# Hybrid decoder block on one core: when roundings, sums, gates and splits are given out in the branch and output stages

## The chip, the core and the metric

The kernel runs on one core of a Trainium2 chip. TensorE (PE in the profile) multiplies, VectorE (DVE), ScalarE (ACT) and GpSimd (POOL) do the elementwise work, and SyncE (SP) issues most transfers; POOL and ACT issue some too. Each engine takes its instructions in order. The metric is the device time of one execution in microseconds; the median of the runs stands for a kernel.

## The reference, cut to what matters

The input of 512 positions gets 16 meta tokens in front and a layer norm. One projection gives ten groups of 1024 columns: queries, keys, values and gates of two attention branches, and a merge gate for each. After the attentions:

```python
br_d = einsum('blw,wd->bld', y_d * silu(g_d), w_br_diff[i])
br_s = einsum('blw,wd->bld', y_s * silu(g_s), w_br_sb[i])
merged = sigmoid(m_d + b_gate[i, 0]) * br_d + sigmoid(m_s + b_gate[i, 1]) * br_s
y = einsum('bld,de->ble', merged, w_out[i])
h = layer_norm(DN_ALPHA * h + y, ln_g[i], ln_b[i])
return h[:, N_META:]
```

Everything is float32, 1024 wide. The attentions and their projections come first and take some 526 us; the change is behind them.

## The kernel before

**Products in two halves.** TensorE multiplies rounded operands (type fp32r). Each float32 operand is therefore split into a rounded part (ACT casts it) and the remainder (DVE subtracts), and a product is three matmuls: high by high, low by high, high by low. For weights these are `wh` and `wl`, a "half" of 128x512 each. `hi(h)` casts and `lo(h)` subtracts half number h; `prep(h)` does both, and each step of the products calls it for the half that is four ahead (AHEAD = 4). `fetch` has SP load raw weights as ring buffers come free (6 of `raw`, 4 of `rawa`).

**Gates.** A merge gate `md` j or `ms` j is one product of 24 matmuls of 512 columns (two halves of weights), then a sigmoid on ACT. MD and MS are the results, 128x512 each, j = 0 to 7.

**Branch products.** Each branch is computed two output blocks at a time by a scheme with seven products in place of eight: a "pair" BD p (differential branch) or BS p (stick-breaking), p = 0 to 3. A product has 12 matmuls of 256 columns. The operands are seven combinations of quarters of y, built in four parts by `operands` (results `gh` and `gl`, sums in `t`); the weights need five loads per pair, two with a second matrix added while it is loaded (POOL's accumulating transfers into `rawa`), and two sums on DVE. `pair` accumulates products in PSUM bank x, copies x away on ACT in between (u, then w), and DVE combines them (c11, c22, c21) and multiplies with the gate. PE may write x again only when it has been copied or read.

**Merge.** `merged(j)` adds MD to MS on DVE, casts the sum (`mh`, ACT), subtracts (`ml`, DVE). It is called at the end of the products of BS p for j = 2p + 1 and 2p.

**Output.** `split_out(c, k)` splits 128 rows of w_out for column half c into `wo0h`/`wo0l` or `wo1h`/`wo1l`. For each half and each of four position blocks t, 24 matmuls of 512 columns give `pso` (the last block in two of 256). DVE builds the residual in `hr` (two instructions a block and half, from x loaded once more), adds pso, takes statistics, and normalizes after the second half. `load_half` loads x and the vectors into the buffers of wh and wl.

**Order.** In these stages the order of each engine, SP's too, is that of the program text: `keep_order` chains them. `seq` fixes the order of products; `run(products, steps)` inserts other work at given points of progress, in rough us. Before, it was: md3 to md7, BD0 to BD3, ms0 to ms3, BS0, ms4, BS1, ms5, ms6, ms7, BS2, BS3, output. Lines that the steps of the prediction touch: L162 `wh`, L167 `wl`, L153 `sum`, L139 accumulating transfers, L856 to L862 operands, L884 u, L892 c22, L917 to L921 merge, L927 and L928 w_out, L960 and L961 residual, L985 addition, L450 to L452 gates, L879 pairs, L982 to L984 output.

Of the kernel before, what the change touches and what calls it, by code (L numbers as in the profile page):

```python
# [43 lines left out]
def hybrid_block_kernel(ctx: ExitStack, tc: tile.TileContext, x, meta, emb_g, emb_b, w_in, b_gate,  # L44
# [24 lines left out]
    for u, (kind, n) in enumerate(UNITS):  # L69
        if u + 1 < len(UNITS):  # L70
# [39 lines left out]
    raws, split, adds = {}, [], []  # L110
    rings = {False: ("raw", 6, []), True: ("rawa", 4, [])}
    state = {"l": 0, "h": 0, "sum": None, "n": 0}
# [6 lines left out]
    def fetch(most=99):  # L119

        while state["l"] < len(loads) and most:
            l = state["l"]
            src, more = loads[l]
            tag, bufs, log = rings[more is not None]
            if len(log) >= bufs and left[log[-bufs]] or (more is not None) not in pools:
                return
            raw = pools[more is not None].tile([P, 4, P], F32, tag=tag, name=tag, bufs=bufs)
            nc.sync.dma_start(raw if l < WOUT else raw.rearrange("p a b -> p (a b)"), src)
            if more is not None:
                adds.append((state["n"], l, more))  # L130
            raws[l] = raw
            log.append(l)
            state["l"] += 1
            most -= 1

    def add_up(now):
        while adds and (now is None or adds[0][0] <= now):
            _, l, more = adds.pop(0)
            g.dma_start(raws[l], more, accum_op=ALU.add)  # L139

    def hi(h):

        assert len(split) == h
        item = items[h]
        for l in item if isinstance(item, tuple) else [item]:
            assert l not in [l for _, l, _ in adds], "not added up yet"
        if item is None:
            raw = raw0[:, h // 2, ts(h % 2, 4)]
        elif isinstance(item, tuple):
            first, second = item  # L150
            one = state["sum"] if first is None else raws[first]
            raw = one if first is None else pools[True].tile([P, 4, P], F32, tag="sum", name="sum", bufs=2)
            v.tensor_tensor(raw, one, raws[second], op=ALU.add)  # L153
            for l in item:
                if l is not None:
                    left[l] -= 1
            state["sum"] = raw
        else:
            raw = raws[item]
        wh, wl = [wpool.tile([P, 4, P], F32R, tag=w, name=w, bufs=6) for w in ("wh", "wl")]  # L160
        split.append((raw, wh, wl))
        s.copy(wh, raw)  # L162
# [685 lines left out]
    def operands(y):  # L848


        gh, gl = [lp.tile([P, 7, 4, 256], F32R, tag=n, name=n) for n in ("gh", "gl")]

        def part(i):
            a, b = y[:, i, :], y[:, i + 4, :]
            t = [lp.tile([P, 256], F32, tag="tmp", name="t", bufs=8) for n in range(4)]
            v.tensor_tensor(t[0], a[:, LEFT], a[:, RIGHT], op=ALU.subtract)  # L856
            v.tensor_tensor(t[2], a[:, RIGHT], b[:, RIGHT], op=ALU.subtract)
            v.tensor_tensor(t[1], t[2], a[:, LEFT], op=ALU.subtract)
            v.tensor_tensor(t[3], t[1], b[:, LEFT], op=ALU.add)
            for n, src in enumerate((a[:, LEFT], b[:, LEFT], b[:, RIGHT], *t)):  # L860
                s.copy(gh[:, n, i, :], src)
                v.tensor_tensor(gl[:, n, i, :], src, gh[:, n, i, :].bitcast(F32), op=ALU.subtract)  # L862

        return (gh, gl), [lambda i=i: part(i) for i in range(4)]

    def pair(kind, p, G, t, done):
# [5 lines left out]
        u, z7, w, c11, c22, c21 = [lp.tile([P, 256], F32, tag="tmp", name="t", bufs=8) for n in range(6)]  # L872
# [35 lines left out]
    SS = ypool.tile([P, KT, S], F32, tag="yd", name="ss")  # L908
# [5 lines left out]
    def merged(j):  # L914

        t = SS[:, j, :]
        v.tensor_tensor(t, t, MD[j], op=ALU.add)  # L917
        pool, tag, bufs = (gpool, "sg", 6) if j < 3 else (lp, "td", 5)
        MH[j] = pool.tile([P, S], F32R, tag=tag, name="mh", bufs=bufs)
        s.copy(MH[j], t)  # L920
        v.tensor_tensor(ML[:, j, :], t, MH[j].bitcast(F32), op=ALU.subtract)  # L921
# [10 lines left out]
    for p in range(4):  # L932
        steps = []
        if p == 2:
            run([merge_gate(1, j, SS[:, j, :]) for j in (6, 7)])
        if p == 3:
            WO = [[hpool.tile([P, KT, 512], F32R, tag=f"hT{x}", name=f"wo0{x}") for x in "hl"]]
            steps = [(1.5 + 1.2 * k, lambda k=k: split_out(0, k)) for k in range(6)]
        run([pair("BS", p, G, [SS[:, 2 * p + m, :] for m in range(2)], lambda m, p=p: merged(2 * p + m))], steps)
        if p < 2:  # L940
            run([merge_gate(1, 4 + p, SS[:, 4 + p, :])])

# [19 lines left out]

    load_half(0)
    for k in range(6, KT):
        split_out(0, k)
    load_half(1)
    residual(0, 0)
    WO.append([lp.tile([P, KT, 512], F32R, tag=f"g{x}", name=f"wo1{x}") for x in "hl"])
    lgb = ypool.tile([P, 2, D], F32, tag="yd", name="lgb")
    nc.scalar.dma_start(lgb[:, 0, :], ln_g[0].partition_broadcast(P))  # L970
    nc.scalar.dma_start(lgb[:, 1, :], ln_b[0].partition_broadcast(P))
    sts = [lr.tile([P, 4, 6], F32, tag="fst", name="fst", bufs=4) for t in range(NB)]
    for c in range(2):
        for t in range(NB):
            st, final = sts[t], t == NB - 1
            for o, w in [(0, 256), (256, 256)] if final and c else [(0, 512)]:
                r, hr = ds(o, w), hrs[t][c]
                ps = pj.tile([P, 512], F32, tag="pj", name="pso")[:, :w]
                for n, k in enumerate((0, 1, 2, 3, 4, 5, 7, 6)):
                    mh, ml = MH[k][:, ts(t, P)], ML[:, k, ts(t, P)]  # L980
                    wh, wl = WO[c][0][:, k, r], WO[c][1][:, k, r]
                    pe.matmul(ps, mh, wh, start=(n == 0), stop=False)  # L982
                    pe.matmul(ps, mh, wl, start=False, stop=False)
                    pe.matmul(ps, ml, wh, start=False, stop=(n == KT - 1))  # L984
                v.scalar_tensor_tensor(hr[:, r], hr[:, r], DN_ALPHA, ps, op0=ALU.mult, op1=ALU.add)  # L985
# [64 lines left out]
```

## Time and profile before

| | |
|---|---|
| median of three runs | 749.88 us (746.13 to 750.96) |
| profiled execution, its own time | 746.05 us |
| its span | 744.2 us |
| mean granted TensorE clock | 0.995 |
| bytes read / written | 67.32 / 2.10 MB |

The page gives for each engine its busy time and share of the span. A window row gives the same for a stretch. A timeline row reads: start, duration, engine, line, operation, output <- inputs, shapes, count, and in brackets how long the engine was idle before it and what ended that. "wh", "q" and the like are the program's tile names. A releaser is what came last by the profile; the engine may have been held in turn by something else, which its own rows show.

### The profile page before, as it was taken

How to read it: one execution, taken by the hardware profiler on the slowest of the kernel's cores; microseconds unless marked ns; L12 is line 12 of the kernel's file. 1: busy time of each engine (PE TensorE's matmuls, PEld its weight loads, DVE VectorE, ACT ScalarE, POOL GpSimd, SP SyncE). 2: the span in 40 equal slices, each digit the busy share in tenths (PEclk: the TensorE clock that was granted, in tenths of full speed). 3: DMA queues.
4: the chain of work that ended last, by engine and by line, in shares of the span. 5: the costliest groups of instructions: out<-in, count | busy, mean ns of one | idle time of the engine just before them, and what ended most of it. 6: DMA issues, size and time to landing. Idle time of an engine off the chain costs nothing.

```text
span 744.2 us, 13129 instructions
## 1 busy us (share of the span) xinstructions
PE 722.2 (97%) x4658; PEld 659.0 (89%) x4658; DVE 586.1 (79%) x1342; ACT 448.6 (60%) x1131; POOL 85.1 (11%) x110
## 2 busy tenths in 40 slices
PE   9999999999999999999999999999999999998985
PEld 8999999999999897989999999988878989997765
DVE  6798778877785699796969696976498898748697
ACT  5686777877776776665657575665375564444300
POOL 3310111011000000000000100110022011110002
PEclk9999999999999999999999999999999999999999
DMA  9142221222213222222222231222188484563802
GB/s 273 51 119 81 62 82 47 69 58 85 66 50 85 71 72 57 57 86 57 72 72 78 65 86 58 78 64 85 44 155 183 102 198 100 141 144 119 291 15 100
DMA packets 120483, 70.27 MB, mean 94 GB/s; under 512 B 4145, under 2 KB 114898, under 8 KB 120418
## 3 DMA queue, kind: packets, MB, share of 16 engines
q1 hardware_dynamic: 111650, 64.18, 29.6%
q0 software_dynamic: 8448, 4.20, 4.6%
q10 hardware_dynamic: 320, 1.06, 0.4%
q8 instruction: 37, 0.61, 0.3%
q14 instruction: 28, 0.23, 0.1%
HBM read 67.32 MB, written 2.10 MB: 93 GB/s over the span
## 4 chain that ended last, share of the span: by engine, by line
PE 84%; DVE 10%; DMA 2%; issue 1%; ACT 1%; POOL 1%; SPq 0%; DVEq 0%; ACTq 0%; POOLq 0%
PE ps L466 23%; PE ps L450 10%; PE ps L451 10%; PE ps L452 10%; PE q L879 10%; PE sc L608 4%; PE t L621 3%; DMA hr<-in_x_dram 2%; DVE wl L167 1%; PE t L626 1%; PE bank L341 1%; DVE gl L862 1%; PE av L784 1%; PE tv L571 1%; PE av L785 1%
## 5 line engine op out<-in xcount | busy, mean ns | idle before, releaser
L167 DVE TENSOR_TENSOR wl<-raw,wh 128x512 fp32r<-128x512 f32 x180 | 125.7, 705 | 38.0 <-ACT wh L162 35.9
L466 PE MATMUL ps<-hTh,wh 128*128 128x264 f32 x512 | 147.1, 287 | 0.0
L466 PE MATMUL ps<-hTl,wh 128*128 128x264 f32 x512 | 146.4, 286 | 0.0
L466 PE MATMUL ps<-hTh,wl 128*128 128x264 f32 x512 | 146.0, 285 | 0.0
L452 PE MATMUL ps<-hTh,wl 128*128 128x512 f32 x368 | 144.5, 393 | 1.1 <-DVE wl L167 1.1
L450 PE MATMUL ps<-hTh,wh 128*128 128x512 f32 x368 | 144.7, 393 | 0.1
L451 PE MATMUL ps<-hTl,wh 128*128 128x512 f32 x368 | 144.6, 393 | 0.0
L162 ACT CAST wh<-raw 128x512 fp32r<-128x512 f32 x180 | 110.0, 620 | 46.8 <-PE ps L451 36.0
L466 PEld LDWEIGHTS ps<-hTh,wh 128*128 128x128 f32 x512 | 96.4, 188 | 1.3
L466 PEld LDWEIGHTS ps<-hTl,wh 128*128 128x128 f32 x512 | 96.5, 188 | 0.9
L466 PEld LDWEIGHTS ps<-hTh,wl 128*128 128x128 f32 x512 | 96.4, 188 | 0.3
L452 PEld LDWEIGHTS ps<-hTh,wl 128*128 128x128 f32 x368 | 69.2, 188 | 15.1 <-DVE wl L167 1.5
L450 PEld LDWEIGHTS ps<-hTh,wh 128*128 128x128 f32 x368 | 69.2, 188 | 13.8 <-ACT wh L162 0.6
L451 PEld LDWEIGHTS ps<-hTl,wh 128*128 128x128 f32 x368 | 69.2, 188 | 12.9
L879 PE MATMUL q<-gh,wh 128*128 128x256 f32 x224 | 64.4, 287 | 5.2 <-ACT t L884 5.2
L879 PE MATMUL q<-gh,wl 128*128 128x256 f32 x224 | 64.2, 287 | 0.3 <-DVE wl L167 0.3
L879 PE MATMUL q<-gl,wh 128*128 128x256 f32 x224 | 64.0, 286 | 0.0
L632 DVE TENSOR_TENSOR al<-t,ah 128x512 fp32r<-128x512 f32 (+2 forms) x88 | 45.9, 526 | 19.9 <-ACT ah L631 13.5
L770 DVE TENSOR_TENSOR_SCAN om<-om 128x528 f32<-128x528 f32 (+2 forms) x64 | 55.0, 868 | 6.8 <-ACT om L766 6.4
L631 ACT CAST ah<-t 128x512 fp32r<-128x512 f32 (+2 forms) x88 | 39.9, 463 | 28.8 <-PE t L621 23.3
L608 PE MATMUL sc<-k,A 128*128 128x264 f32 (+2 forms) x256 | 56.5, 308 | 0.2 <-POOL k L525 0.2
L879 PEld LDWEIGHTS q<-gh,wh 128*128 128x128 f32 x224 | 43.7, 195 | 5.9 <-ACT t L884 5.6
(238 smaller groups left out, 1431.8 us busy)
## 6 DMA issues: line engine op xcount, KB each, us to landing
raw<-in_w_in_dram SPq DMA_DIRECT2D x152, 256.0 KB, 3.0
raw<-in_w_out_dram SPq DMA_DIRECT2D x16, 256.0 KB, 3.4
raw<-in_w_br_diff_dram SPq DMA_DIRECT2D x12, 256.0 KB, 3.8
raw<-in_w_br_sb_dram SPq DMA_DIRECT2D x12, 256.0 KB, 4.6
raw<-in_w_in_dram SPq DMA_DIRECT2D x4, 512.0 KB, 6.5
rawa<-in_w_br_diff_dram SPq DMA_DIRECT2D x8, 256.0 KB, 3.5
rawa<-in_w_br_diff_dram POOLq DMA_DIRECT2D x8, 256.0 KB, 5.8
rawa<-in_w_br_sb_dram SPq DMA_DIRECT2D x8, 256.0 KB, 4.4
```

The costliest lines, as they stand in the source:

```text
L162: s.copy(wh, raw)
L167: eng.tensor_tensor(wl, raw, wh.bitcast(F32), op=ALU.subtract)
L450: pe.matmul(ps, wh[:, k % 4, :], hTh[:, k, M:], start=(k == 0), stop=False)
L451: pe.matmul(ps, wh[:, k % 4, :], hTl[:, k, M:], start=False, stop=False)
L452: pe.matmul(ps, wl[:, k % 4, :], hTh[:, k, M:], start=False, stop=(k == KT - 1))
L466: pe.matmul(ps[:, :H2], a[:, k % 4, :], b[:, k, ts(c, H2)], start=(k == 0 and m == 0), stop=(k == KT - 1 and m == 2))
L608: pe.matmul(ps[:, :n], q, K[:, m, k0:k0 + n], start=(m == 0), stop=(m == 1))
L621: pe.transpose(t[:, o:o + P], a[:, AOFF[i] + j * P:AOFF[i] + (j + 1) * P], ident)
L631: s.copy(h, t[:, o:o + w])
L632: v.tensor_tensor(l, t[:, o:o + w], h.bitcast(F32), op=ALU.subtract)
L770: v.tensor_tensor_scan(rev, rev, rev, 1.0, ALU.mult, ALU.min)
L879: pe.matmul(bank, a[:, k, :], b[:, n, k, :], start=start and k == 0 and m == 0, stop=k == 3 and m == 2, skip_group_check=not start)
```

## The change

It does six things, all behind the attentions.

1. ms0 and ms1 move ahead of BD0; ms2 to ms6 stand ahead of BS0; BS0, BS1 and BS2 follow each other; ms7 stands between BS2 and BS3.
2. `operands` builds the four sums in one tile and casts and subtracts in three instructions of 256, 512 and 1024 columns instead of seven of 256; its four parts are spaced over seven gates (five in the second branch) instead of five (four). The pairs use slices of the same kind of tile.
3. The sums of weights (`add`) are computed one step before the half is cast.
4. For j below 6 the branch sum is an accumulating transfer on POOL's queue; its cast comes six steps of `prep` later and the remainder one more, from a list `later`. For j = 6 and 7 DVE adds, and the cast comes one step later.
5. Of the first half of w_out, five splits stand in BS3 (six before) and three behind it (two before).
6. In the output stage, splits of the second half and residuals are given out by a table, ahead of the addition of the block; the transfers of ln_g and ln_b are issued after the first block's splits.

```diff
-    seq += [("md", j) for j in range(3, 8)] + [("BD", p) for p in range(4)] + [("ms", j) for j in range(4)]
-    seq += [x for p in range(4) for x in ([("BS", p), ("ms", 4 + p)] if p < 2 else [("ms", 6), ("ms", 7), ("BS", 2)]
-                                          if p == 2 else [("BS", 3)])]
+    seq += [("md", j) for j in range(3, 8)] + [("ms", 0), ("ms", 1)] + [("BD", p) for p in range(4)]
+    seq += [("ms", j) for j in range(2, 7)] + [("BS", p) for p in range(3)] + [("ms", 7), ("BS", 3)]
...
+    def add(h):
+
+        first, second = items[h]
+        one = sums.pop(True) if first is None else raws[first]
+        raw = one if first is None else pools[True].tile([P, 4, P], F32, tag="sum", name="sum", bufs=2)
+        v.tensor_tensor(raw, one, raws[second], op=ALU.add)
...
     def prep(h):
         state["n"] += 1
-        add_up(state["n"] - 1)
         if h < len(items):
             hi(h)
             lo(h)
+        if h + 1 < len(items) and isinstance(items[h + 1], tuple):
+            add(h + 1)
         fetch()
+        while later and later[0][0] <= state["n"]:
+            later.pop(0)[1]()
...
-            for n, src in enumerate((a[:, LEFT], b[:, LEFT], b[:, RIGHT], *t)):
-                s.copy(gh[:, n, i, :], src)
-                v.tensor_tensor(gl[:, n, i, :], src, gh[:, n, i, :].bitcast(F32), op=ALU.subtract)
+            for o, src in ((slice(0, 1), a[:, LEFT].unsqueeze(1)), (slice(1, 3), b.rearrange("p (a n) -> p a n", a=2)),
+                           (slice(3, 7), t)):
+                s.copy(gh[:, o, i, :], src)
+                v.tensor_tensor(gl[:, o, i, :], src, gh[:, o, i, :].bitcast(F32), op=ALU.subtract)
...
-    run([merge_gate(0, j, MD[j]) for j in range(3, 8)], [(0.3 + 5.4 * i, f) for i, f in enumerate(parts)])
+    run([merge_gate(0, j, MD[j]) for j in range(3, 8)] + [merge_gate(1, j, early_ms[j]) for j in range(2)],
+        [(0.3 + 7.5 * i, f) for i, f in enumerate(parts)])
...
-    run([merge_gate(1, j, SS[:, j, :]) for j in range(4)], [(0.3 + 4.8 * i, f) for i, f in enumerate(parts)])
+    run([merge_gate(1, j, MS[j]) for j in range(2, 7)], [(0.3 + 5.5 * i, f) for i, f in enumerate(parts)])
...
     def merged(j):
-        t = SS[:, j, :]
-        v.tensor_tensor(t, t, MD[j], op=ALU.add)
-        pool, tag, bufs = (gpool, "sg", 6) if j < 3 else (lp, "td", 5)
-        MH[j] = pool.tile([P, S], F32R, tag=tag, name="mh", bufs=bufs)
-        s.copy(MH[j], t)
-        v.tensor_tensor(ML[:, j, :], t, MH[j].bitcast(F32), op=ALU.subtract)
+        wait = 6 if j < 6 else 1
+        if j < 6:
+            g.dma_start(MS[j], MD[j], accum_op=ALU.add)
+        else:
+            v.tensor_tensor(MS[j], MS[j], MD[j], op=ALU.add)
+        later.append((state["n"] + wait, lambda: rounded(j)))
+        later.append((state["n"] + wait + 1, lambda: rest(j)))
+        later.sort(key=lambda x: x[0])
...
-            steps = [(1.5 + 1.2 * k, lambda k=k: split_out(0, k)) for k in range(6)]
+            steps = [(0.8 + 1.6 * k, lambda k=k: split_out(0, k)) for k in range(5)]
...
-    residual(0, 0)
-    nc.scalar.dma_start(lgb[:, 0, :], ln_g[0].partition_broadcast(P))
-    nc.scalar.dma_start(lgb[:, 1, :], ln_b[0].partition_broadcast(P))
+    MEANWHILE = [[lambda: residual(0, 0)] + [lambda k=k: split_out(1, k) for k in range(3)],
+                 [lambda: residual(1, 0)] + [lambda k=k: split_out(1, k) for k in range(3, 6)],
+                 [lambda: residual(2, 0)] + [lambda k=k: split_out(1, k) for k in range(6, 8)] + [lambda: residual(0, 1)],
+                 [lambda: residual(3, 0)] + [lambda t=t: residual(t, 1) for t in range(1, 3)],
+                 [lambda: residual(3, 1)], [], [], []]
...
+                if o == 0:
+                    for work in MEANWHILE[NB * c + t]:
+                        work()
+                    if t == 0 and c == 0:
+                        nc.scalar.dma_start(lgb[:, 0, :], ln_g[0].partition_broadcast(P))
+                        nc.scalar.dma_start(lgb[:, 1, :], ln_b[0].partition_broadcast(P))
...
             if c == 0:
-                split_out(1, 2 * t)
-                split_out(1, 2 * t + 1)
-                if t + 1 < NB:
-                    residual(t + 1, 0)
-                residual(t, 1)
                 continue
```

Here `rounded(j)` is the cast of MS[j] to `mh` and `rest(j)` the remainder `ml`, as they stood in `merged` before.

**ACT, from the end of BS2 into BS3.** Before:

```order
L162 CAST wh<-sum 128x512
L920 CAST mh<-ss 128x512
L162 CAST wh<-raw 128x512
L920 CAST mh<-ss 128x512
L162 CAST wh<-rawa 128x512
L884 COPY t<-q 128x256
```

With the change, from the last two weight casts in BS2 through ms7 into BS3:

```order
L153 CAST wh<-sum 128x512
L153 CAST wh<-raw 128x512
L485 ACTIVATE ss<-ps,cols 128x512
L153 CAST wh<-rawa 128x512
L936 CAST wo0h<-raw 128x512
L880 COPY t<-q 128x256
L153 CAST wh<-raw 128x512
L936 CAST wo0h<-raw 128x512
L882 COPY t<-q 128x256
L153 CAST wh<-sum 128x512
L916 CAST mh<-ss 128x512
```

The copy u (L884 before, L880 now) no longer has the two casts of BS2's sums ahead of it; the first of them stands ten rows lower, and the first cast of w_out stands right ahead of u.

**DVE, from the last branch sum to the second block's residual.** `hr` is the residual, L960 and L966 its first instruction, L985 and L1002 the addition of the product. Before:

```order
L917 TENSOR_TENSOR ss<-ss,td 128x512
L921 TENSOR_TENSOR ml<-ss,mh 128x512
L928 TENSOR_TENSOR wo0l<-raw,wo0h 128x512 x2
L960 SCALAR_TENSOR_TENSOR hr<-hr,xmv,eg 128x512
L961 SCALAR_TENSOR_TENSOR hr<-hr,xrs,eb 128x512
L985 SCALAR_TENSOR_TENSOR hr<-hr,pso 128x512
L988 BN_STATS fst<-hr 128x6
L928 TENSOR_TENSOR wo1l<-raw,wo1h 128x512 x2
```

With the change:

```order
L927 TENSOR_TENSOR ss<-ss,td 128x512
L919 TENSOR_TENSOR ml<-ss,mh 128x512 x2
L937 TENSOR_TENSOR wo0l<-raw,wo0h 128x512 x3
L966 SCALAR_TENSOR_TENSOR hr<-hr,xmv,eg 128x512
L967 SCALAR_TENSOR_TENSOR hr<-hr,xrs,eb 128x512
L937 TENSOR_TENSOR wo1l<-raw,wo1h 128x512 x3
L1002 SCALAR_TENSOR_TENSOR hr<-hr,pso 128x512
L1005 BN_STATS fst<-hr 128x6
```

Three splits of the second half now stand ahead of the first block's addition, where two stood behind it.

**POOL, in the branch stages.** Before there are, behind the attentions' last gates, the sixteen accumulating transfers of weights and then the normalization:

```order
L481 TENSOR_TENSOR ysT<-sg,ysT 128x512 x2
L139 DMA rawa<-in_w_br_diff_dram 128x4x128 x8
L139 DMA rawa<-in_w_br_sb_dram 128x4x128 x8
L261 TENSOR_TENSOR lne<-fmv,epsr 128x1
L262 TENSOR_TENSOR frs<-lne,neghalf 128x1
```

With the change (`sm` and `ss` are MS, `sm` and `td` on the right MD):

```order
L129 DMA rawa<-in_w_br_diff_dram 128x4x128 x8
L129 DMA rawa<-in_w_br_sb_dram 128x4x128 x6
L925 DMA sm_6827<-sm_6702 128x512
L925 DMA sm_6826<-sm_6629 128x512
L129 DMA rawa<-in_w_br_sb_dram 128x4x128 x2
L925 DMA ss<-td 128x512
L925 DMA ss<-sm_6768 128x512
L925 DMA ss<-td 128x512 x2
```

Six transfers from one on-chip tile to another come in, the first two between the weight transfers of BS2 and those of BS3.

More of the change, by code (lines that the diff above doesn't have):

```diff
@@ L109, in hybrid_block_kernel @@
     raw0 = ypool.tile([P, 4, KT, P], F32, tag="ys", name="raw0")
-    raws, split, adds = {}, [], []
+    raws, split, sums, later = {}, [], {}, []
     rings = {False: ("raw", 6, []), True: ("rawa", 4, [])}
-    state = {"l": 0, "h": 0, "sum": None, "n": 0}
+    state = {"l": 0, "h": 0, "n": 0}
     pools = {False: wpool}
@@ L129, in fetch @@
             if more is not None:
-                adds.append((state["n"], l, more))
+                g.dma_start(raw, more, accum_op=ALU.add)
             raws[l] = raw
@@ L134, in fetch @@
             most -= 1
[L136 to L139, printed above, removed]
+    def add(h):
[3 more added lines that the diff above has]
+        v.tensor_tensor(raw, one, raws[second], op=ALU.add)
+        for l in items[h]:
+            if l is not None:
+                left[l] -= 1
+        sums[h] = sums[True] = raw
     def hi(h):
@@ L144, in hi @@
         item = items[h]
[L145 to L159, printed above, removed]
+        raw = raw0[:, h // 2, ts(h % 2, 4)] if item is None else sums.pop(h) if isinstance(item, tuple) else raws[item]
         wh, wl = [wpool.tile([P, 4, P], F32R, tag=w, name=w, bufs=6) for w in ("wh", "wl")]
@@ L871, in pair @@
         x, z, y = [pool.tile([P, 512], F32, tag=tag, name="q")[:, :256] for pool, tag in of]
-        u, z7, w, c11, c22, c21 = [lp.tile([P, 256], F32, tag="tmp", name="t", bufs=8) for n in range(6)]
+        tmp = lp.tile([P, 4, 256], F32, tag="tmp", name="t", bufs=2)
+        u, z7, w = c11, c22, c21 = [tmp[:, n, :] for n in range(3)]
         def product(q, bank, n, start=True):
```

32 lines of the change are left out of this document (19 added, 13 removed).

## The prediction

> **What bounds the kernel.** I read the page's engine table first, then windows by stage, then PE's timeline for every wait, and last ACT's and DVE's timelines around each.
>
> ```profile
> PE 722.2 (97%) x4658; PEld 659.0 (89%) x4658; DVE 586.1 (79%) x1342; ACT 448.6 (60%) x1131; POOL 85.1 (11%) x110
> ```
> PE is busy 97% of the span, and the change issues the same matmuls; only holes and slow stretches of PE can be won. All rows up to about 526 us stay in their order, so I look behind that. Columns of the next table, of windows: stretch in us, its length, PE busy (instructions), granted clock, DMA share, GB/s.
>
> ```profile
> 555.19:598.05 42.86, 40.81 (x337) 1.00 0.68 148
> 620.00:630.07 10.07, 10.07 (x86) 1.00 0.45 131
> 630.07:635.54 5.47, 5.47 (x27) 1.00 0.01 3
> 661.79:687.35 25.56, 22.07 (x169) 0.93 0.31 100
> 678.40:682.60 4.20, 4.20 (x22) 0.59 0.39 133
> 687.35:736.18 48.83, 44.73 (x218) 1.00 0.42 142
> 718.28:720.00 1.72, 1.72 (x8) 1.00 0.00 0
> ```
> An undisturbed pair (BS0, second row) takes 10.07 us, an undisturbed gate 5.47. By these, BD0 to BD3 (first row) lost 42.86 - 4 x 10.07 = 2.58. BS2 and BS3 (fourth) lost 25.56 - 20.14 = 5.42. The output product has seven blocks of 24 matmuls of 512 columns, as a gate has, and 48 of 256 columns, so it needs 7 x 5.47 + 48/84 x 10.07 = 44.04 and lost 4.79. The holes are these, by PE's timeline (start, duration, instruction, idle before and its releaser):
>
> ```profile
> 541.90 0.50 PE L452 MATMUL ps<-hTh,wl 128*128 128x512 f32 x1 [1.10 <-DVE wl L167]
> 557.33 0.39 PE L879 MATMUL q<-gh,wl 128*128 128x256 f32 x1 [0.30 <-DVE wl L167]
> 560.52 0.39 PE L879 MATMUL q<-gh,wh 128*128 128x256 f32 x1 [1.74 <-ACT t L884]
> 678.38 0.39 PE L879 MATMUL q<-gh,wh 128*128 128x256 f32 x1 [3.49 <-ACT t L884]
> 692.37 0.50 PE L982 MATMUL pso<-wo0h,mh 128*128 128x512 f32 x1 [0.75 <-ACT wo0h L927]
> 693.26 0.50 PE L983 MATMUL pso<-wo0l,mh 128*128 128x512 f32 x1 [0.39 <-DVE wo0l L928]
> 718.28 0.50 PE L983 MATMUL pso<-wo1l,mh 128*128 128x512 f32 x1 [2.97 <-DVE wo1l L928]
> ```
>
> **A. Two more gates ahead of BD0, fuller operand instructions.** DVE was the bound from 536 to 560: it took one operand part and two weight remainders (wl) in turn without a pause.
>
> ```profile
> 542.37 0.42 DVE L856 TENSOR_TENSOR t<-ydT 128x256 f32<-128x256 f32 x1
> 543.96 1.09 DVE L862 TENSOR_TENSOR gl<-ydT,gh 128x256 fp32r<-128x256 f32 x3
> 544.97 1.43 DVE L862 TENSOR_TENSOR gl<-t,gh 128x256 fp32r<-128x256 f32 x4
> 546.31 1.29 DVE L167 TENSOR_TENSOR wl<-raw,wh 128x512 fp32r<-128x512 f32 x2
> 555.25 1.43 DVE L862 TENSOR_TENSOR gl<-t,gh 128x256 fp32r<-128x256 f32 x4
> ```
> A part takes 546.31 - 542.37 = 3.94 us, two wl 1.2, together 5.14 against PE's 5.47 per gate. The last part ended at 556.6, behind BD0's start at 555.19; hence the holes at 557 and 560. The gates ms0 and ms1 now give PE 2 x 5.47 = 10.9 us more before BD0. Seven gl of 256 columns (2.35 us) become one of 256, 512 and 1024: at 0.34 per 256 and 0.60 per 512 (pitches of these rows) some 2.07 as an estimate, so DVE gains 0.3 a part, and ends about 9 us ahead of BD0. Both holes go: +2.6 (bounds 0 and +2.58). The hole at 541.9 hangs on the first part, which still stands ahead of its wl; the single 1024-wide cast must now end before the last gl starts, which I price at -0.2 (0 to -0.5).
>
> **B. Roundings given out later, ms2 to ms6 ahead of BS0.** In BS2, ACT stood in order behind casts (mh) that waited for a sum made on DVE at that moment; PE waited for the copy queued behind them:
>
> ```profile
> 673.88 0.62 ACT L920 CAST mh<-ss 128x512 fp32r<-128x512 f32 x1 [2.28 <-DVE ss L917]
> 676.92 0.62 ACT L920 CAST mh<-ss 128x512 fp32r<-128x512 f32 x1 [1.90 <-DVE ss L917]
> 677.45 0.61 ACT L162 CAST wh<-rawa 128x512 fp32r<-128x512 f32 x1
> 677.97 0.36 ACT L884 COPY t<-q 128x256 f32<-128x256 f32 x1
> ```
> In the new order no mh waits for a sum of the same moment in BS0 to BS2, and ms7 (5.47 us of cover) stands between BS2 and BS3. The hole of 3.6 and the slow clock behind it (0.59 over 4.20 us, 1.7 us) both go: +5.4 (bounds 0 and +5.42). [...]
>
> The additions themselves: six DVE adds of 0.6 leave DVE, and six accumulating transfers of 256 KB come to POOL's queue. The trace has accumulating transfers of the same size (from DRAM, though); duration min/median/max in ns, and landing:
>
> ```profile
> L139 POOL DMA_DIRECT2D rawa<-in_w_br_sb_dram x8: 1282/1282/1837, 601.9 to 656.9; - x8
> DMA to landing us min/median/max: 3.3/4.8/7.5
> ```
> The cast stands six weight steps behind the multiply, five products of 1.44 = 7.2 us, so 7.5 is about covered; and behind the cast the next copy that PE needs is five products away. I take 0, with its price as a rival. POOL's queue holds nothing else in this stretch but the weight sums of BS2 and BS3, which are loaded a pair ahead.
>
> **C. Output.** Three w_out splits are left for after BS3 instead of two, the second half's splits move ahead in DVE's order, and the residuals spread. The limit here is DVE, which starts when the first x rows land:
>
> ```profile
> 695.00 0.75 DVE L960 SCALAR_TENSOR_TENSOR hr<-hr,xmv,eg 128x512 f32<-128x512 f32 x1 [1.79 <-DMA hr<-in_x_dram]
> 703.27 0.75 DVE L960 SCALAR_TENSOR_TENSOR hr<-hr,xmv,eg 128x512 f32<-128x512 f32 x1 [2.56 <-DMA hr<-in_x_dram]
> 704.73 0.68 DVE L985 SCALAR_TENSOR_TENSOR hr<-hr,pso 128x512 f32<-128x512 f32 x1
> 706.05 1.28 DVE L928 TENSOR_TENSOR wo1l<-raw,wo1h 128x512 fp32r<-128x512 f32 x2
> 707.25 0.75 DVE L960 SCALAR_TENSOR_TENSOR hr<-hr,xmv,eg 128x512 f32<-128x512 f32 x1
> 708.70 0.75 DVE L960 SCALAR_TENSOR_TENSOR hr<-hr,xmv,eg 128x512 f32<-128x512 f32 x1
> 719.75 0.69 DVE L985 SCALAR_TENSOR_TENSOR hr<-hr,pso 128x512 f32<-128x512 f32 x1
> 730.63 0.69 DVE L985 SCALAR_TENSOR_TENSOR hr<-hr,pso 128x512 f32<-128x512 f32 x1 [0.32 <-PE pso L984]
> 706.33 1.28 ACT L927 CAST wo1h<-raw 128x512 fp32r<-128x512 f32 x2 [4.89 <-DMA raw<-in_w_out_dram]
> ```
> Times from here on count with BS3's end at 687.35, as before. PE's hole at 692 shrinks from 1.6 to about 0.55 (the third split ends near 692.1, the matmul wants it at 691.7), so PE could end the fifth block at 687.35 + 0.55 + 5 x 5.47 = 715.25. But DVE must do, from 695.0 to that block's addition, eight residuals of 1.45 (707.25 to 708.70), eight wo1l of 0.60 (two from 706.05 to 707.25) and four additions with statistics of 1.32 (704.73 to 706.05): 21.7 us, to 716.7 at best. Before it was 719.75: +3.0, and 0.3 more, since DVE no longer waits for PE at 730.63. I take +3.2. Bounds: if DVE still waits 2.56 for a transfer (hr, or w_out 6 and 7, which landed at 706.3), +0.7; if x lands early enough that PE leads, 4.79 - 0.55 = +4.2. The tail behind the last addition is unchanged.
>
> **Sum.** 2.6 - 0.2 + 5.4 + 3.2 = 11.0: the span goes from 744.2 to 733.2. The profiled execution took 746.05, 1.85 more than its span: 735.1. Its own time lies at the low end of the three runs (746.13 to 750.96) and 3.8 below their median of 749.88; the trace does not say what the other two spent. I add half of it, 1.9: 737.0.
>
> **Rivals.**
> 1. *DVE too full in BS1 and BS2*, which now follow BS0 without a gate. A BD pair from c22 to c22 shows the load:
>
> ```profile
> 575.26 0.41 DVE L892 TENSOR_TENSOR t<-t,q 128x256 f32<-128x256 f32 x1
> 577.71 0.69 DVE L167 TENSOR_TENSOR wl<-sum,wh 128x512 fp32r<-128x512 f32 x1 [0.76 <-ACT wh L162]
> 582.68 0.69 DVE L167 TENSOR_TENSOR wl<-sum,wh 128x512 fp32r<-128x512 f32 x1 [0.74 <-ACT wh L162]
> 585.29 0.42 DVE L892 TENSOR_TENSOR t<-t,q 128x256 f32<-128x256 f32 x1 [0.20 <-PE q L879]
> ```
> 10.03 us with 1.70 idle, and two remainders (ml) of 0.6 come in: 9.55 of 10.07. This fits if the waits of 0.75 on ACT go, as the sum given one step earlier should make them; if they stay it is 11.05, 1 us a pair over two pairs: 739.0.
> 2. *Output still waits for transfers*. The bytes are the same, and the DMA engines were full (the last two columns are DMA share and GB/s):
>
> ```profile
> 692.00:704.00 12.00, 11.24 (x48) 9.11 (x49) 7.43 (x12) 3.75 (x7) 0.00 (x0) 1.00 1.03 367
> ```
> +0.7 in place of +3.2: 739.5.
> 3. *The hole at BS3 only changes its holder*: ACT now casts wo0h of w_out 0 ahead of the copy in BS3. For it: casts on w_out rows waited 4.89 above. Against: its load is free to start in BS2. The 5.4 stay: 742.4.
> 4. *Slower: the new transfers land late.* Past 7.2 + about 5 = 12 us PE waits for each of three pairs; 11 us of gain are eaten at 12 + 11/3 = 15.7, and 1% is lost from 18 on: 757. Against it stands the longest landing, 7.5. [...]
>
> **Chances.** Forecast 0.52, rivals 0.17, 0.17, 0.07 and 0.07. A measurement of this kernel can tell about 1% from no change, 742.4 to 757.4. Below lie the forecast and the first two, less 0.10 for both together or a slow execution: 0.76. Within: that 0.10 and rival 3: 0.17. Above: rival 4. The range 733 to 743 takes in the sum at its best (C at +4.2, nothing added to the profiled time: 734.1) and 1 us of scatter below it, and rivals 1 to 3; it leaves out rival 4 and part of the mixed cases.
>
> **What would show it.** Right: no PE wait on the copy u in BS0 to BS3, clock 1.00 there, four BD pairs in 40.3 us, and the output at 45 to 46 us with DVE without a pause up to the fifth block's addition. Wrong: an mh cast waiting for a transfer over 5 us, c22 late on DVE in BS1 or BS2, or hr or wo1h waits above 2 us.

## The result and the profile after

| | before | after |
|---|---|---|
| median of the runs side by side | 749.61 us (746.13 to 750.96, 4 runs) | 738.17 us (736.24 to 738.55, 4 runs) |
| ratio | | 0.985 [0.981, 0.989] |
| profiled execution, its span | 746.05, 744.2 us | 738.30, 736.5 us |

The kernel became 1.5% faster, by 11.4 us between the medians; 737.0 had been forecast. The engine line of the page after:

```profile
PE 721.0 (98%) x4658; PEld 658.0 (89%) x4658; DVE 579.1 (79%) x1304; ACT 445.3 (60%) x1099; POOL 90.2 (12%) x116
```

TensorE has as many matmuls as before and is busy for 98% of a shorter span. Its waits behind 525 us, from the view of waits of the kernel after (waiting line, releaser, total us, times, longest):

```profile
PE ps L444 <- ACT wh L153: 0.6, 1, 0.6
PE ps L446 <- DVE wl L158: 0.6, 1, 0.6
PE pso L994 <- DVE wo0l L937: 0.6, 2, 0.3
PE q L875 <- ACT t L884: 0.2, 1, 0.2
```

Of the 10.7 us of waits that the prediction's rows list, 2.0 are left, none on the copy u (L884 is the copy w in this kernel; u is L880). The stages come from windows on TensorE's own starts (stretch, its length, PE busy, granted clock, DMA share, GB/s): first the stretch up to BD0 of before, then the kernel after from there to the end.

```profile
534.52:555.19 20.67, 19.43 (x84) 1.00 0.66 140
```

```profile
535.97:567.51 31.54, 30.31 (x132) 1.00 0.63 144
567.51:607.83 40.32, 40.32 (x338) 1.00 0.64 143
607.83:635.05 27.22, 27.22 (x122) 1.00 0.79 174
635.05:665.29 30.24, 30.24 (x254) 1.00 0.87 175
670.75:681.33 10.58, 10.39 (x86) 1.00 0.51 157
681.33:736.50 55.17, 44.76 (x218) 0.93 0.38 144
```

The rows after are the gates up to BD0, the four BD pairs, the five gates behind them, BS0 to BS2, BS3, and the output stage, whose mean clock takes in an end without matmuls: up to 728.5 us it is 1.00. The gate ms7, from 665.29 to 670.75, has no row here. With the ends of before (BD0 at 555.19, its end at 598.05, the output stage from 687.35 to 744.2) the account is this; a gate costs 5.47 us, as in the prediction:

| stretch | before | after | gain |
|---|---|---|---|
| start to the last gates | 534.52 | 535.97 | -1.45 |
| gates up to BD0 | 20.67 | 31.54, two gates more | +0.07 |
| four BD pairs (A) | 42.86 | 40.32 | +2.54 |
| gates behind them, BS0 to BS3 (B) | 89.30 | 73.50, two gates less | +4.86 |
| output stage (C) | 56.85 | 55.17 | +1.68 |
| sum | 744.20 | 736.50 | +7.70 |

A is there within 0.1 us, B nearly, C at half its size. And a stretch in which the two programs are the same lost 1.45 us.

### The profile page after: what moved, and what is told of

The parts are those of the page before. It is cut to its first block, busy times and chain, and to the rows that moved or that the text cites. A ratio compares the mean times of both kernels' runs of the same rounds, so it can differ in the third digit from the quotient of the medians.

```text
span 736.5 us, 13070 instructions
## 1 busy us (share of the span) xinstructions
PE 721.0 (98%) x4658; PEld 658.0 (89%) x4658; DVE 579.1 (79%) x1304; ACT 445.3 (60%) x1099; POOL 90.2 (12%) x116
## 4 chain that ended last, share of the span: by engine, by line
PE 85%; DVE 8%; DMA 3%; issue 1%; ACT 1%; POOL 1%; SPq 0%; DVEq 0%; POOLq 0%; ACTq 0%
PE ps L460 23%; PE ps L444 11%; PE ps L446 11%; PE ps L445 11%; PE q L875 10%; PE sc L602 4%; PE t L615 3%; DMA raw<-in_w_out_dram 2%; PE t L620 1%; PE bank L335 1%; PE av L778 1%; PE tv L565 1%; PE av L779 1%; DMA eb<-in_emb_ln_b_dram 1%; DVE hr L1019 1%
## 5 line engine op out<-in xcount | busy, mean ns | idle before, releaser
L760 ACT ACTIVATE om<-sc 128x264 f32<-128x264 f32 (+3 forms) x80 | 31.7, 396 | 24.7 <-DVE sc L757 23.1
```

The lines of the kernel that those rows point to most:

```text
L760: s.activation(om[:, o], ps[:, :use], AF.Sigmoid, scale=-1.0)
```

## Experiments

Each kernel is the changed one with one edit unless said otherwise. Differences are against the changed kernel, whose second set of runs gave 737.47; the ratios are to the kernel before, run beside each. The runs came in three sets, in which the kernel before gave 750.71, 749.47 and 749.28 us; so up to 1.4 us between runs of different sets need not be a difference between kernels. The first set is branch sums, rounding at once, gates behind BD and old output order; the last is the first part later and the row below it.

| run | median us (lowest to highest, runs) | ratio to before |
|---|---|---|
| changed again | 737.47 (736.67 to 738.60, 6) | 0.984 [0.982, 0.987] |
| branch sums on VectorE | 738.97 (738.06 to 739.81, 4) | 0.986 [0.983, 0.988] |
| rounding at once | 744.01 (742.66 to 745.18, 4) | 0.992 [0.990, 0.995] |
| gates behind BD | 742.48 (739.94 to 743.23, 4) | 0.991 [0.988, 0.994] |
| old output order | 741.51 (740.32 to 741.71, 4) | 0.989 [0.986, 0.991] |
| two gates between pairs | 738.92 (738.38 to 739.90, 5) | 0.986 [0.983, 0.988] |
| rounding 2 products later | 747.69 (746.95 to 749.59, 12) | 0.999 [0.997, 1.000] |
| splits first | 735.98 (734.87 to 737.48, 6) | 0.982 [0.980, 0.984] |
| first part later | 735.89 (735.07 to 736.71, 5) | 0.981 [0.979, 0.984] |
| the last two and a split order | 732.80 (732.42 to 734.48, 5) | 0.978 [0.975, 0.980] |

### The same programs again: what differs between two executions

> The changed kernel itself, unaltered, as the measure for the other runs on the same chip and to see how far two executions of one program differ. 736 to 739.5 us. If the 1.45 us that its first profile lost between 290 and 310 us (granted clock 0.91 there) belong to that execution, this profile may have the last unit's addition at 535.4 us as the kernel before has, in place of 536.8; if they belong to the program, it is 536.8 again.

> The kernel before, unaltered, for a second profile of it. The first profile's execution took 746.05 us, below the median of 749 to 750. Theory (the executions of the kernel before differ by what the clock does behind its holes, above all behind the 2.97 us at the fifth block of the output stage, which had a granted clock of 1.00 behind it in that profile and 0.72 in the run with the old output order): this profile has the same holes within 0.3 us and a span of 745 to 750 us, with a clock below 0.9 behind one that was followed by 1.00. Rival (the holes themselves differ in size from execution to execution): another hole, or one longer by over 1 us.

The second execution of the changed kernel took 736.67 us (span 734.9). Its stages, as windows, and a stretch of 4 us in the part that no edit touches:

```profile
534.40:565.94 31.54, 30.31 (x132) 1.00 0.67 148
565.94:606.25 40.31, 40.31 (x337) 1.00 0.62 140
606.25:679.75 73.50, 73.31 (x482) 1.00 0.78 172
679.75:734.90 55.15, 44.79 (x218) 0.94 0.39 144
292.00:296.00 4.00, 4.00 (x19) 1.00 0.00 0
```

The same stretch in the first profile of the changed kernel:

```profile
292.00:296.00 4.00, 4.00 (x12) 0.57 0.00 0
```

All stages of the change repeat within 0.02 us. The 1.45 us are those four microseconds at a clock of 0.57, where 12 matmuls start in place of 19: they belong to the execution, not to the change. Ahead of them stands a short hole, by TensorE's timeline of the first profile:

```profile
291.57 0.34 PE L779 MATMUL av<-al,V 128*128 128x160 f32 x1 [1.14 <-DVE al L626]
```

TensorE is idle for the same 1.14 us of the 20 us from 290 to 310 in the first profile of before and in the second of the changed kernel (18.86 us busy in all three), in a part that no edit touches, and from 292 to 296 the clock is 1.00 in both of these. The sixteen instructions of one line of that part (L783, L789 in the kernel before) take 252.8 to 252.9 us from the first start, at 284, to the last in four profiles (this one, branch sums on VectorE, two gates between pairs, first part later) and 251.4 in the first of before and in the seven others of the changed kernel and its edits. Between the two profiles that lost nothing there, the change is worth 744.2 - 734.9 = 9.3 us of span, not 7.7.

The kernel before was run again too, for one profile: 749.56 us, span 747.8. Its holes stand where they stood. What differs is the clock behind them. Behind the hole of 1.74 us in BD0, first in the first profile of before, then in the second:

```profile
560.52:564.00 3.48, 3.48 (x29) 1.00 0.48 126
```

```profile
560.63 0.53 PE L879 MATMUL q<-gh,wh 128*128 128x256 f32 x1 [1.74 <-ACT t L884]
555.30:599.65 44.35, 42.30 (x337) 0.96 0.64 141
560.63:564.00 3.37, 3.37 (x16) 0.51 0.56 157
720.25 0.50 PE L983 MATMUL pso<-wo1l,mh 128*128 128x512 f32 x1 [3.35 <-DVE wo1l L928]
688.94:747.80 58.86, 46.53 (x218) 0.95 0.39 131
720.25:729.25 9.00, 9.00 (x32) 0.81 0.15 58
```

The hole is 1.74 us in both, to the hundredth, and behind it the clock is 1.00 in one and 0.51 in the other: 44.35 - 42.86 = 1.49 us. The output's hole, 2.97 us in the first profile with 1.00 behind it (the row 718.28 of the prediction), is 3.35 here with 0.81 behind it, and the stage takes 58.86 - 56.85 = 2.01 us longer. These two make 3.5 of the 3.6 us between the spans, and about the distance of the first profiled execution from the median. The expectation is met, apart from the hole that is 0.38 longer.

### B: what took the hole at BS3 away

```
 def merged(j):
-    wait = 6 if j < 6 else 1
-    if j < 6:
-        g.dma_start(MS[j], MD[j], accum_op=ALU.add)
-    else:
-        v.tensor_tensor(MS[j], MS[j], MD[j], op=ALU.add)
+    v.tensor_tensor(MS[j], MS[j], MD[j], op=ALU.add)
-    later.append((state["n"] + wait, lambda: rounded(j)))
-    later.append((state["n"] + wait + 1, lambda: rest(j)))
-    later.sort(key=lambda x: x[0])
+    rounded(j)
+    rest(j)
```

> The changed kernel with the branch sums on VectorE and the rounding given out at once behind the sum, as before the change; everything else as changed. Theory (the rounding that stands ahead of the next pair's copy u on ScalarE was the cause of the holes): a hole of 3 to 4 us at the second or third product of BS1 and of BS2, which now follow one another without a gate, none at BS3 since a gate stands ahead of it, with a granted clock below 1.00 behind each: 4 to 9 us above the changed kernel, 742 to 747 us. Rival (gates in place of pairs are what counts, or VectorE's load): no hole on copy u, at most 1 us more than the changed kernel.

6.5 us slower, as the theory had it, and with no hole on u at BS3. BS0 to BS2 as a whole, the matmuls behind the holes at BS1 and BS2, and the clock behind the first, in this kernel:

```profile
633.91:671.91 38.00, 33.70 (x253) 0.91 0.53 119
649.24 0.38 PE L875 MATMUL q<-gh,wh 128*128 128x256 f32 x1 [2.22 <-ACT t L880]
649.24:654.00 4.76, 4.76 (x27) 0.64 0.46 136
663.14 0.39 PE L875 MATMUL q<-gh,wh 128*128 128x256 f32 x1 [2.08 <-ACT t L880]
```

The three pairs take 38.00 us in place of 30.24. The releaser is the copy u in both, and ScalarE's timeline shows who held it:

```profile
647.78 0.62 ACT L916 CAST mh<-sm 128x512 fp32r<-128x512 f32 x1 [1.90 <-DVE sm L923]
648.83 0.36 ACT L880 COPY t<-q 128x256 f32<-128x256 f32 x1
```

The cast mh waited 1.90 us for its sum, and the copy that TensorE needs stood behind it. The holes, 2.1 to 2.2 us, are smaller than the 3 to 4 expected; of the 7.8 us that the pairs lost, 4.3 are holes and the rest is the clock behind them (0.65 over 4.86 us behind the second).

The first half of that edit alone, with the rounding still six products later:

> The changed kernel with one part undone: all eight branch sums are additions on VectorE (0.6 us each) and none is an accumulating transfer; the rounding is still given out six products later. Theory (the later rounding is what took the wait at copy u away, the transfers only spare VectorE): 738 to 739 us, at most 0.5 us above the changed kernel, TensorE without a wait on copy u in BS0 to BS3 and the three pairs BS0 to BS2 within 30.2 to 30.8 us. Rival (VectorE is too full in BS1 and BS2 without the transfers): about 1 us for each of BS1 and BS2, 740 us or more, with TensorE waiting for VectorE's operands or differences there.

No wait on the copy u. But BS0 to BS2 took 1.04 us more than with the transfers, outside the 30.2 to 30.8 expected, with one hole, at BS2, by TensorE's timeline of this kernel:

```profile
634.92:666.20 31.28, 30.49 (x254) 1.00 0.64 144
661.78 0.38 PE L875 MATMUL q<-gh,wh 128*128 128x256 f32 x1 [0.79 <-ACT t L884]
```

VectorE's and ScalarE's timelines of the same kernel show why:

```profile
655.99 0.69 DVE L924 TENSOR_TENSOR ss<-ss,td 128x512 f32<-128x512 f32 x1
658.25 0.69 DVE L924 TENSOR_TENSOR ss<-ss,sm 128x512 f32<-128x512 f32 x1
660.06 0.69 DVE L140 TENSOR_TENSOR sum<-sum,raw 128x512 f32<-128x512 f32 x1
660.84 0.62 ACT L153 CAST wh<-sum 128x512 fp32r<-128x512 f32 x1 [2.31 <-DVE sum L140]
```

Two additions of the branch sums delay the weight's sum, its cast waits 2.31 us for that, and the copy w stands behind the cast. So VectorE was too full in one pair of the two that the rival named. The transfers take this away. The median is 0.8 and 1.5 us above the two sets of the changed kernel, where at most 0.5 had been expected; the ratios don't tell the two kernels apart, and the 1.04 us is a reading of one profile. This kernel and the one that rounds at once differ only in when the rounding is given out: 744.01 - 738.97 = 5.0 us.

How close the transfers come:

```
-        wait = 6 if j < 6 else 1
+        wait = 2 if j < 6 else 1
```

> The changed kernel with the rounding given out two products behind the accumulating transfer (about 2.8 us) in place of six (about 8.4 us). Theory (a transfer takes 3.7 to 6.8 us to land, and the casts that stand ahead of copy u wait for it): ScalarE waits 2 to 5 us for a transfer at each cast of BS0 to BS2, TensorE has holes of 1 to 4 us on copy u in BS1 and BS2, and the time is 3 to 9 us above the changed kernel. Rival (the transfers are so quick that the distance does not matter): within 0.7 us of it.

10.2 us slower than the changed kernel, more than the 3 to 9 expected; the kernel is back at before. ScalarE's and TensorE's timelines at BS2:

```profile
663.62 0.62 ACT L916 CAST mh<-ss 128x512 fp32r<-128x512 f32 x1 [6.72 <-DMA ss<-td]
664.56 0.58 PE L875 MATMUL q<-gh,wh 128*128 128x256 f32 x1 [4.47 <-ACT t L880]
```

The cast waited 6.72 us for a transfer, the copy u stood behind it, and TensorE waited 4.47 us for u (1.87 in BS1). In the changed kernel, with six products between, two such casts still waited, 1.10 and 1.07 us, which cost TensorE nothing there (ScalarE's timeline for the first; then POOL's instructions and the landings, in ns and us, from the view of the transfers' line):

```profile
662.26 0.62 ACT L916 CAST mh<-ss 128x512 fp32r<-128x512 f32 x1 [1.10 <-DMA ss<-td]
```

```profile
L925 POOL DMA_DIRECT2D ss<-td x3: 856/856/1827, 656.5 to 668.2; - x3
DMA to landing us min/median/max: 3.3/4.3/6.8
```

The last line holds for all six transfers. So six products don't quite cover the longest landing of 6.8 us; the rest is hidden because ScalarE's next copy for TensorE, u of BS3, comes only at 672.57.

Last for B, the gates' places:

```
-    seq += [("ms", j) for j in range(2, 7)] + [("BS", p) for p in range(3)] + [("ms", 7), ("BS", 3)]
+    seq += [("ms", j) for j in range(2, 6)] + [("BS", 0), ("ms", 6), ("BS", 1), ("ms", 7), ("BS", 2), ("BS", 3)]
```

The two `run` calls follow this order, and the operand parts come every 4.8 us.

> The changed kernel with two gates between pairs again: ms2 to ms5 ahead of BS0 with operand parts every 4.8 us, ms6 between BS0 and BS1, ms7 between BS1 and BS2, and BS2 and BS3 one behind the other, as the product order before had it. Theory (it is the later rounding that counts, not where the gates stand): within 0.7 us of the changed kernel, no wait on copy u above 0.5 us in BS3. Rival (a gate ahead of BS3 is what keeps copy u in time): a hole of 2 to 3.5 us at BS3 and 2 to 5 us in all above the changed kernel.

Between 0.75 and 1.45 us above the two sets of the changed kernel, a little more than the 0.7 expected; the ratios don't tell the kernels apart. There is no wait on the copy u; two of 0.33 and 0.92 us on c22 (VectorE) are new, the longer at BS3, which here follows BS2 without a gate. The later rounding is what counts, and the gate ahead of BS3 is worth 1.5 us at most.

### A: the gates ahead of BD0

```
-    seq += [...] + [("ms", 0), ("ms", 1)] + [("BD", p) for p in range(4)]
+    seq += [...] + [("BD", p) for p in range(4)] + [("ms", 0), ("ms", 1)]
```

with the operand parts every 5.4 us in five gates, as before, and seven gates behind BD.

> The changed kernel with the gates ms0 and ms1 behind the four BD pairs again (five gates with operand parts every 5.4 us ahead of BD, seven gates behind it). Theory (the two gates gave the operands time): the four BD pairs take 42 to 43 us in place of 40.3, and the whole is 2 to 2.6 us longer than the changed kernel, 740 to 741 us. Rival (the fuller operand instructions alone did it): BD stays at 40.3 to 41 us and the time within 0.7 us of the changed kernel.

5.0 us slower than the second set, 4.3 than the first, where 2 to 2.6 had been expected. The four BD pairs and the hole in BD0 in this kernel:

```profile
555.13:598.29 43.16, 41.12 (x337) 1.00 0.66 146
560.46 0.39 PE L875 MATMUL q<-gh,wh 128*128 128x256 f32 x1 [1.74 <-ACT t L880]
```

The hole of 1.74 us is back, and BD is 2.84 us longer, with the fuller operand instructions kept: the gates' time is all of A, the instructions nothing. That the median lost more than the profile shows would fit the clock behind this same hole, seen at 0.51 above: this profile has 1.00 there and a mean clock of 0.995, the three other executions have 0.990 to 0.992. Where they lost it no trace shows, so it is argued, not shown.

### C: the output stage

The order of before in the output stage (splits and residuals behind each block's addition, six splits in BS3, `lgb` loaded first):

```
             if c == 0:
+                split_out(1, 2 * t)
+                split_out(1, 2 * t + 1)
+                if t + 1 < NB:
+                    residual(t + 1, 0)
+                residual(t, 1)
                 continue
```

> The changed kernel with the order of the output stage before the change: two splits and two residuals behind each block's addition, six splits in BS3, the LayerNorm rows loaded ahead of all. Theory as in the prediction (VectorE's order bounds the stage, +3.2 us): 741 us. Theory from the changed kernel's trace (the gain there was 1.8 us, since the split of the sixth and seventh output weight waits 2.2 us for its load): 739.5 to 740.3 us, the fifth block's addition some 34 to 36 us behind the stage's start in place of 31.4. Rival (the gain lies elsewhere): within 0.5 us of the changed kernel.

741.51 is near the 741 of the first theory and above the 739.5 to 740.3 of the second. But the fifth block's addition came 32.81 us behind the stage's start, not 34 to 36, so VectorE's order is not all of it. The stage, the hole and the clock behind it in this kernel:

```profile
680.58:739.80 59.22, 47.51 (x218) 0.89 0.37 131
710.85 0.80 PE L992 MATMUL pso<-wo1l,mh 128*128 128x512 f32 x1 [3.31 <-DVE wo1l L937]
710.85:720.50 9.65, 9.65 (x30) 0.68 0.14 54
```

Without the slow clock behind its hole the first profile of before had 56.85 for this stage; here, and at 58.86 in the second profile of before, the hole costs 2.0 to 2.4 us more. C is worth 1.7 us in an execution whose clock stays up and about 4 in one where it falls.

Why 1.7 and not 3.2, VectorE, ScalarE and SyncE of the changed kernel show in their timelines:

```profile
688.68 0.75 DVE L966 SCALAR_TENSOR_TENSOR hr<-hr,xmv,eg 128x512 f32<-128x512 f32 x1 [1.91 <-DMA hr<-in_x_dram]
701.58 1.34 DVE L937 TENSOR_TENSOR wo1l<-raw,wo1h 128x512 fp32r<-128x512 f32 x2 [2.22 <-ACT wo1h L936]
712.77 0.68 DVE L1002 SCALAR_TENSOR_TENSOR hr<-hr,pso 128x512 f32<-128x512 f32 x1
700.93 1.26 ACT L936 CAST wo1h<-raw 128x512 fp32r<-128x512 f32 x2 [5.11 <-DMA raw<-in_w_out_dram]
695.25 0.85 SPq L127 DMA_DIRECT2D raw<-in_w_out_dram  x2
728.66 0.40 DVE L1002 SCALAR_TENSOR_TENSOR hr<-hr,pso 128x256 f32<-128x256 f32 x1
```

VectorE began 681.33 + 7.35, as early as the prediction wanted, but waited 2.22 us for the splits of rows 6 and 7, whose weights landed late: SyncE issued them at 695.25, behind the four loads of x for the second half (from 690.92). TensorE has no wait left in the second half. Its last matmul starts at 726.37, 45.04 us behind the stage's start, in place of 736.06, 48.71; that is 3.7 us won. But VectorE's last addition (728.66) starts 2.3 us behind that matmul, before 0.4 (736.45), and the stage ends with VectorE. The edit that tests this gives out three splits ahead of the second half's loads and of the first residual:

```
-    load_half(1)
     WO.append(...)
+    for k in range(3):
+        split_out(1, k)
+    load_half(1)
...
-    MEANWHILE = [[lambda: residual(0, 0)] + [lambda k=k: split_out(1, k) for k in range(3)],
+    MEANWHILE = [[lambda: residual(0, 0)],
```

> The changed kernel with the first three splits of the second half of the output weight moved ahead of the second half's loads and of the first residual, so that VectorE works while it waited 1.9 us for hr, and so that the loads of the sixth and seventh weight row are issued before the second half's rows. Theory (the output stage now ends late because VectorE is 2 to 3 us behind TensorE, of which 2.2 us is the wait for that split): the wait at the split of rows 6 and 7 falls below 0.5 us, the fifth block's addition comes 28.5 to 30 us behind the stage's start in place of 31.4, and the time is 1 to 2.5 us below the changed kernel. Rival (the transfers are limited together, and whatever is issued first makes another late: hr or the second half): within 0.5 us, with a new wait of about 2 us on hr.

1.5 us faster, within the expectation. The stage and VectorE's timeline in this kernel:

```profile
679.93:733.20 53.27, 44.78 (x218) 0.95 0.43 149
693.79 1.38 DVE L937 TENSOR_TENSOR wo1l<-raw,wo1h 128x512 fp32r<-128x512 f32 x2 [0.79 <-ACT wo1h L936]
708.99 0.68 DVE L1004 SCALAR_TENSOR_TENSOR hr<-hr,pso 128x512 f32<-128x512 f32 x1
```

The wait at rows 6 and 7 is gone (waits of 0.54 and 0.79 us remain, on rows 3 to 5), and the fifth block's addition comes 708.99 - 679.93 = 29.06 us behind the stage's start in place of 31.44. The stage is 55.15 - 53.27 = 1.88 us shorter: this wait was what C lacked.

### The hole at the first operand part, and all together

```
-        [(0.3 + 7.5 * i, f) for i, f in enumerate(parts)])
+        [(3.5 + 7.5 * i, f) for i, f in enumerate(parts)])
```

> The changed kernel with the four operand parts for BD given out 3.2 us later each (3.5, 11.0, 18.5, 26.0 in place of 0.3, 7.8, 15.3, 22.8). Theory (the holes of about 0.6 us at each of the two products at 541 to 543 us come from the first part, which stands ahead of that gate's weight on ScalarE and VectorE): both holes go, the stage up to BD is 1.0 to 1.3 us shorter, 736.2 to 737 us against 737.5. Rival (the holes only move to the next weight): the same time within 0.4 us.

1.6 us faster, slightly more than expected. The stretch up to BD0 in this kernel:

```profile
536.22:565.95 29.73, 29.73 (x132) 1.00 0.73 158
```

29.73 in place of 31.54 with no wait left: the two holes were 1.81 us in all, 1.24 of waits and 0.58 of longer busy time (30.31 against 29.73).

The last kernel takes both edits and gives out the three splits ahead of the output product in TensorE's order:

```
-    for k in range(5, KT):
+    for k in (5, 7, 6):
         split_out(0, k)
```

> The run with the splits first, the later operand parts of the other run, and the last three splits of the first half of the output weight in the order 5, 7, 6 in which TensorE takes them. Theory (the three losses lie one behind the other on TensorE's path): 1.5 us for the splits as measured, 1.0 to 1.3 us for the operand parts, 0.3 to 0.6 us for the order, in sum 734 to 735 us against 737.5 for the changed kernel. Rival (they share a cover, the output stage then waits for hr's load since it begins earlier against the loads): 735.3 to 736.5 us.

732.80 us, 4.7 below the changed kernel and better than expected; 0.978 [0.975, 0.980] of before, an interval that does not meet the changed kernel's. Behind 525 us its TensorE waits half a microsecond in all, 0.3 for `wo0l` and 0.2 for the copy w; with the order 5, 7, 6 one of the two waits for `wo0l` is gone.

### What the runs leave open

A, B and C undone one at a time cost 5.0, 6.5 and 4.0 us, 15.5 together, more than the 12.0 between the kernels in the second set (749.47 - 737.47). So these prices are not shares of the gain: the kernel that rounds at once has two holes where the kernel before has one, and the clock behind a hole comes and goes (1.00 and 0.51 behind the same 1.74 us). Two parts of the change are undone in no run: the weights' sums one step earlier (point 3 of the change), and the weights' accumulating transfers, which `fetch` now issues at once, where before they came one step later; the six points do not name the second.

## Why the prediction came out right, step by step

- **A, +2.6.** Measured 2.54. The reason holds too: with the gates behind BD, the same hole of 1.74 us is back. The 0.3 us a part that the fuller instructions were to add played no part.
- **The hole at 541.9, -0.2.** It became two of 0.62, and the stretch as a whole gained 0.07. The mechanism was read rightly, as the kernel with the first part later shows; the size was off by 0.3.
- **B, +5.4.** Measured 4.86. BS3 kept half a microsecond (10.58 against 10.07), with a wait of 0.19 on w. The step that failed slightly is "both go": a small part of the hole changed its holder, as in rival 3, which is hereby answered with 0.5 in place of 5.4. On ScalarE the casts that stand right ahead of w there are a weight's sum, an mh and a wo0h; in the kernel that rounds at once, without the mh, this wait is not there. That the later rounding is the cause is shown by that kernel, against the one with the branch sums on VectorE.
- **The transfers, 0.** Right as a price on the path. But they were not just moved work: without them BS2 lost 1 us to the mechanism of rival 1. And the margin was thin, as the waits of 1.10 and 1.07 us at six products and the 10.2 us lost at two products show. Rival 4's mechanism is real; its point was not reached.
- **C, +3.2.** Measured 1.7. The step that failed is "DVE must do 21.7 us of work, to 716.7 at best": the forecast took VectorE to run without a pause, though the working itself named the wait for w_out 6 and 7 as a bound. It happened, at 2.22 us, in kind as rival 2 had it: a sign that the prediction had named as one of being wrong. The fifth block's addition came 0.96 us earlier in place of 3.0 (31.44 against 32.40 behind the stage's start), and VectorE won 0.8 behind it, up to its last addition, in place of 0.3. The sign of being right, an output of 45 to 46 us, came true on TensorE (45.04 to its last matmul), but VectorE paused and ends the stage 2 us behind it. Taking the wait away gave 1.88 us of the stage back.
- **From the profiled execution to the median, +1.9.** Half of an unexplained difference of 3.8 had been added. The second profile of before shows 3.5 of it as a slow clock behind two holes, at BD0 and in the output, both of which the change removes. So less than that had to be added: the second execution of the changed kernel took 736.67 against a median of 737.47, 0.8 us.

The time came out right because two errors offset each other: the sum of 11.0 was 1.7 too large against 9.3 us of span (1.5 of it C), and the scatter added was 1.1 too large. The mechanisms of A and B held; the closeness of the last digits was luck.

## What to carry to other kernels

On an engine that works in order, as ScalarE does here (a cast that waited 6.72 us held the copy u behind it), look not at how long an instruction takes but at what its operand is waiting for and which copy stands behind it: giving a cast out a few products later cost nothing and won 5 us here (744.01 against 738.97), 6.5 with the sums moved to transfers. Price a hole on TensorE with the clock behind it as a chance: the same hole was worth 1.7 or 3.2 us in two executions, so removing holes can pay more at the median than one profile shows. Where a stage is bound by a chain of work on VectorE, follow each of that chain's loads back to the queue that issues it before calling it free of pauses.

## What was unexpected of the hardware

- The clock fell to 0.51 over 3.4 us behind a hole of 1.74 us in one execution and stayed at 1.00 behind the same 1.74 us in another; behind the 1.14 us near 291 it was 0.57 in one and 1.00 in two others, behind 2.2 us it was 0.64, behind 2.97 us 1.00, behind 3.31 us 0.68. The length of one hole does not decide: two clocks stood behind the same 1.74 us, and the clock was lower behind 1.14 us than behind 2.97. What decides is not shown.
- In the kernel after, an accumulating transfer of 256 KB between two on-chip tiles occupied POOL for 0.86 us at the least and 1.83 at the most and landed 3.3 to 6.8 us later. What stretched the longest is not shown; on TensorE's path it cost nothing that the changed kernel's trace shows.
- A subtraction of 128x256 on VectorE (L851) took 1.51 us beside a multiplication on POOL in the kernel after; the same line took 0.42 at 544.75 and at 549.89, with nothing on POOL. In the kernel before it took 1.53 and with the first part given out later 1.52, each beside the same multiplication of 1.5 us. It makes the first operand part 1.51 - 0.42 = 1.1 us later. With the first part given out later the holes at 542 are gone all the same; whether they would go without it was not tried. That POOL's instruction is what stretches it no run shows; the subtraction ahead of it, which begins at 537.57 and also overlaps it, took 0.42. The two rows, from VectorE's and POOL's timelines of the kernel after:

```profile
537.91 1.51 DVE L851 TENSOR_TENSOR t<-ydT 128x256 f32<-128x256 f32 x1
```

```profile
537.61 1.52 POOL L475 TENSOR_TENSOR ysT<-sg,ysT 128x512 f32<-128x512 f32 x1 [33.65 <-DVE ysT L783]
```
